# Order of the work on the down-projection's combinations: loads on ScalarE's queue, roundings and stores behind those of a weight unit

## The chip, the cores and the metric

The kernel runs on one core of a Trainium2 chip. Its engines are TensorE (PE: matmuls; its weight loads are listed apart as PEld), VectorE (DVE), ScalarE (ACT), GpSimd (POOL) and SyncE (SP), which here only issues transfers. Each engine works through its own instructions in order: an instruction that waits holds up all that stand behind it on that engine, and that includes transfers which an engine issues. The metric is device time in microseconds (us) of one execution.

## The reference

One layer of a streaming encoder over 512 prompt frames and 64 sample frames, model width 2048: a modulated RMSNorm, two recurrent mixers with their projections, a residual, and then the part that matters here, a gated feed-forward network:

```
gate, val = split(h @ w_up)                   # 2048 -> 2 x 5632
act = silu(causal_dwconv(gate) + bias) * val  # width 3
x = x + g2 * (act @ w_down)                   # 5632 -> 2048
```

and a last RMSNorm. Everything is float32.

## The kernel before, in words

**Products.** A float32 product is made of three matmuls in a rounded format: the weight is split into a high part `wh` (ScalarE rounds it, line 1628) and a low part `wl` (VectorE subtracts, line 1629), the activations likewise, and PE adds wh·hi, wh·lo and wl·hi (lines 1722 to 1724). On top of that the two large products of the network use a scheme with seven block products in place of eight (steps c = 0 to 6): each step multiplies one combination of four weight blocks by one combination of four activation blocks.

**Units.** `up` walks through 44 units t of the up-projection (128 output channels of gate and of value each) and then 32 units of the down-projection. An up unit has 7 steps of 24 matmuls, 168 in all; a down unit has 7 steps of 15, 105 in all. `up_prep` makes the weights of a step two steps ahead of its product: it forms the combination on VectorE (the tiles `s`), rounds it on ScalarE and splits it (`up_split`). The buffers of `wh` and `wl` are three deep, so ScalarE can round a weight only once PE is done with the one three back. `up_load` loads the four weight blocks a11, a21, a22, a12 of a unit into tiles `raw` on SP's queue; six of these rotate in the up-projection. `up_out` takes a step's result from PSUM; `up_conv` and `up_act` make the gated activations of a unit one unit later, and store them in DRAM (`actd[t]`, line 1780).

**The combinations.** The first 40 activation tiles feed the down-projection in 20 pairs. While the up-projection runs, `pair_put(p)` loads `actd[2p]` and `actd[2p + 1]` back into tiles `j`, forms four combinations on GpSimd (tiles ta and tb, line 1849), rounds all seven on ScalarE in four instructions (line 1853), makes the low parts on GpSimd (line 1849 again) and stores both parts in DRAM tiles `cd[p]` (lines 1858 and 1859). The down-projection loads them into freed places (`fill`, line 1901), five per step. `pair_put` is a generator: `up` advances it by one piece at chosen steps. A pair begins at step 3 of an even unit and is advanced at 12 of the next 15 steps.

**What sets the order.** The text of the program sets the order in which work is offered; a scheduler then places each instruction on its engine at the place where, by its own estimate of durations, it can go first. `issue_after(x)` pins the instructions inside it behind instruction x where both are on the same engine. In the kernel before, `split_of` (a unit's subtraction on VectorE) is used so, but nothing of `pair_put` is pinned.

**The end.** In the last eight down units `down_end` adds the partial sums on GpSimd (lines 1945 and 1947), scales them by a modulation vector on ScalarE (line 1954) and adds the residual on GpSimd (line 1955), one piece at each of four steps.

In the down-projection four of the six tiles `j` join the rotation of `raw` tiles, which makes ten, and the other two become places for combinations.

## Time and profile before

| | us |
|---|---|
| median of three runs | 2889.24 (2886.13 to 2890.58) |
| the profiled execution | 2888.42 |
| its span in the profile | 2886.7 |
| up-projection, units 3 to 41 | 1338.1 to 2295.8 |
| down-projection, first to last unit | 2341 to 2810 |

In rows of instructions the columns are start, duration, engine, line of the kernel, operation, tiles (out<-in; the numbers of the buffers are left out) and, in brackets, how long the engine had been idle and what ended that. Rows of stretches give for each engine its busy time and the number of its instructions, then TensorE's granted clock, the share of the DMA engines and GB/s.

### The profile page before, as it was taken

Reading aid. Unit: us, or ns where it says so; the run is one execution under the profiler, and the core shown is the slowest. Engines: PE = TensorE matmul, PEld = TensorE weight load, DVE = VectorE, ACT = ScalarE, POOL = GpSimd, SP = SyncE. Lnnn points to the kernel's source line nnn. Section 1 sums busy time; section 2 is a strip of 40 time slices with the busy share of each in tenths; the row PEclk is TensorE's granted clock in tenths of the full one; section 3 lists DMA queues with packets and bytes.
Section 4 is the critical chain, followed back from the end, with each engine's and each line's share of the span. In section 5 each row is a group of like instructions: output and inputs, shape, how many; then the busy total and the mean of one; then the engine's idle time right before and its main releaser. Section 6 shows DMA issues by size and latency. Waiting matters only on the chain.

```text
span 2886.7 us, 52859 instructions
## 1 busy us (share of the span) xinstructions
PE 2771.4 (96%) x20612; PEld 2671.4 (93%) x20612; DVE 2277.2 (79%) x3721; ACT 1307.3 (45%) x2314; POOL 471.7 (16%) x453
## 2 busy tenths in 40 slices
PE   7999999999999999999999999999999999999988
PEld 4799999999989999999999999999999999999987
DVE  4578787787877887678888888888888876888876
ACT  4255555454544342554444444444444444333343
POOL 0001000010000000002323333333323200000340
PEclk9999999999999999999999999999999999999999
DMA  9965445455554577524555545455545574673651
GB/s 306 317 195 162 134 137 148 136 166 160 155 155 124 151 205 210 158 90 146 157 152 150 157 146 166 142 161 148 161 142 160 170 251 151 183 237 104 216 155 66
DMA packets 647197, 478.18 MB, mean 166 GB/s; under 512 B 65929, under 2 KB 574084, under 8 KB 646948
## 3 DMA queue, kind: packets, MB, share of 16 engines
q1 hardware_dynamic: 639604, 473.14, 55.0%
q8 instruction: 162, 2.65, 0.4%
q10 hardware_dynamic: 7344, 1.67, 0.3%
q14 instruction: 87, 0.71, 0.1%
HBM read 397.76 MB, written 76.96 MB: 164 GB/s over the span
## 4 chain that ended last, share of the span: by engine, by line
PE 39%; issue 22%; DVE 20%; DMA 9%; ACT 5%; POOL 5%; SPq 0%; ACTq 0%; DVEq 0%; POOLq 0%
PE g L646 17%; PE g L648 8%; DVE wl L1629 5%; PE bank L2220 4%; DMA actd<-v 4%; ACT wh L1628 2%; DVE acc L2204 2%; POOL j L1849 2%; PE bank L1724 2%; DVE ca L1772 2%; PE bank L1722 2%; PE bank L1723 2%; DVE s L1656 2%; DMA j<-actd 2%; PE bank L2216 1%
## 5 line engine op out<-in xcount | busy, mean ns | idle before, releaser
L1724 PE MATMUL bank<-slot,wl 128*128 128x290 f32 (+1 forms) x3024 | 901.4, 298 | 51.1 <-DVE wl L1629 51.0
L1722 PE MATMUL bank<-slot,wh 128*128 128x290 f32 (+1 forms) x3024 | 902.8, 299 | 3.3 <-ACT wh L1628 1.7
L1723 PE MATMUL bank<-slot,wh 128*128 128x290 f32 (+1 forms) x3024 | 903.4, 299 | 0.0
L1724 PEld LDWEIGHTS bank<-slot,wl 128*128 128x128 f32 x3024 | 576.7, 191 | 66.4 <-DVE wl L1629 66.4
L1722 PEld LDWEIGHTS bank<-slot,wh 128*128 128x128 f32 x3024 | 569.3, 188 | 9.3 <-issue 3.3
L1723 PEld LDWEIGHTS bank<-slot,wh 128*128 128x128 f32 x3024 | 574.2, 190 | 0.1
L646 PE MATMUL g<-hh,wh 128*128 128x288 f32 x2048 | 472.7, 311 | 1.0 <-ACT ts L2204 0.8
L648 PE MATMUL g<-hh,wl 128*128 128x288 f32 x2048 | 442.3, 297 | 1.7 <-DVE wl L1026 1.7
L646 PE MATMUL g<-hl,wh 128*128 128x288 f32 x2048 | 442.3, 297 | 0.0
L1628 ACT ACTIVATE wh<-raw 128x1024 fp32r<-128x1024 f32 (+1 forms) x304 | 279.8, 921 | 326.9 <-PE bank L1723 234.9
L1629 DVE TENSOR_TENSOR wl<-raw,wh 128x1024 fp32r<-128x1024 f32 (+1 forms) x304 | 322.0, 1059 | 95.5 <-ACT wh L1628 93.0
L646 PEld LDWEIGHTS g<-hh,wh 128*128 128x128 f32 x2048 | 325.0, 190 | 21.8 <-issue 15.1
L648 PEld LDWEIGHTS g<-hh,wl 128*128 128x128 f32 x2048 | 330.8, 189 | 5.3 <-issue 3.3
L646 PEld LDWEIGHTS g<-hl,wh 128*128 128x128 f32 x2048 | 330.1, 189 | 3.6 <-issue 2.7
L1629 DVE TENSOR_TENSOR wl<-s,wh 128x1024 fp32r<-128x1024 f32 (+1 forms) x228 | 275.1, 1208 | 65.0 <-ACT wh L1628 64.4
L1628 ACT ACTIVATE wh<-s 128x1024 fp32r<-128x1024 f32 (+1 forms) x228 | 209.7, 921 | 206.3 <-PE bank L1723 74.4
L1849 POOL TENSOR_TENSOR j<-j,j 128x288 f32<-128x288 f32 (+2 forms) x140 | 202.4, 1463 | 225.4 <-DMA j<-actd 218.2
L2204 ACT ACTIVATE wh<-raw 128x1024 fp32r<-128x1024 f32 x135 | 142.7, 1057 | 198.4 <-PE g L646 192.6
L2204 DVE SCALAR_TENSOR_TENSOR acc<-aw,ct,acc 128x512 f32<-128x512 f32 x284 | 201.1, 742 | 4.5 <-DMA aw<-in_w_ada_dram 4.5
L2204 DVE TENSOR_TENSOR wl<-raw,wh 128x1024 fp32r<-128x1024 f32 x135 | 165.0, 1222 | 46.0 <-ACT wh L2204 43.4
L1722 PE MATMUL g<-slot,wh 128*128 128x288 f32 x560 | 168.5, 301 | 8.1 <-DVE slot L1924 7.3
L1723 PE MATMUL g<-slot,wh 128*128 128x288 f32 x560 | 166.0, 297 | 0.0
(341 smaller groups left out, 4071.8 us busy)
## 6 DMA issues: line engine op xcount, KB each, us to landing
raw<-in_w_up_dram SPq DMA_DIRECT2D x176, 512.0 KB
raw<-in_w_in_dram SPq DMA_DIRECT2D x100, 512.0 KB
raw<-in_w_down_dram SPq DMA_DIRECT2D x128, 320.0 KB
aw<-in_w_ada_dram SPq DMA_DIRECT2D x79, 512.0 KB
slot<-cd SPq DMA_DIRECT2D x140, 288.0 KB
cd<-j SPq DMA_DIRECT2D x120, 288.0 KB
xr<-in_w_ada_dram SPq DMA_DIRECT2D x49, 512.0 KB
hraw<-in_w_ada_dram SPq DMA_DIRECT2D x40, 512.0 KB
```

The costliest lines, as they stand in the source:

```text
L646: T.matmul(ps[:, h if bank is None else bank, :n], wh, x[:, h, :n], start=f, stop=False)
L648: T.matmul(ps[:, h if bank is None else bank, :n], wl, ah[:, h, :n], start=False, stop=stop)
L1628: self.nc.scalar.activation(hi, src, AF.Copy)
L1629: self.nc.vector.tensor_tensor(lo, src, hi.bitcast(F32), op=ALU.subtract)
L1656: V.tensor_tensor(s2, g("s1"), g("a11"), op=ALU.subtract)
L1722: T.matmul(ps, wh[:, j], hi, start=(c < 3 and j == 0), stop=False, skip_group_check=True)
L1723: T.matmul(ps, wh[:, j], lo, start=False, stop=False, skip_group_check=True)
L1724: T.matmul(ps, wl[:, j], hi, start=False, stop=(j == n - 1), skip_group_check=True)
L1772: V.scalar_tensor_tensor(ca[:, :578], cb[:, j:j + 578], w, ca[:, :578], op0=ALU.mult, op1=ALU.add)
L1849: minus = lambda out, a, b: G.tensor_tensor(out, a, b, op=ALU.subtract)
L2204: return f(*a, **kw)
L2220: return self.engine.matmul(out, *a, **kw)
```

## The change

Six things are altered.

1. The loads of a pair go on ScalarE's DMA queue, two whole tiles in place of one whole and two halves on SP's queue. They are pinned behind the rounding that was offered last (`round_of`).
2. A pair begins one unit later, at step 1 of an odd unit, with its loads. The four combinations follow at step 2, and the roundings and stores at steps 1, 2, 4, 5 and 6 of the even unit after it (`PAIR_STEPS`).
3. Each of the four roundings is pinned behind the rounding of a unit's weight that was offered last, and each store behind the last weight load (`load_of`). Rounding and subtraction are offered for r0 and r1 first, then ta, then tb.
4. The rounded parts get tiles of their own (j4, j5, j6; the high part of r0 goes into the second half of r0), so `j` has seven tiles and not six. In the down-projection two of them join the `raw` tiles, which makes eight in place of ten, and five become places for combinations.
5. With fewer `raw` tiles, the load of blocks a11 and a21 two units ahead is offered at step 5 and not at step 3 of a down unit.
6. In `down_end` the residual is loaded in two pieces without its gap, so that one addition on GpSimd does for both pieces; the scalings on ScalarE are pinned behind the last rounding.

```
-            if t + 2 < N_UNITS:
-                self.up_load(t + 2, ("a11", "a21"))
         elif c == 4: ...
         elif c == 5:
...
+            if t + 2 < N_UNITS:
+                self.up_load(t + 2, ("a11", "a21"))
...
-                self.raws[0:0] = [(self.xp, f"j{n}") for n in range(4)]
-                self.vacant += [(self.xp, f"j{n}") for n in (4, 5)]
+                self.raws[0:0] = [(self.xp, f"j{n}") for n in range(2)]
+                self.vacant += [(self.xp, f"j{n}") for n in range(2, 7)]
...
-                if t % 2 == 0 and 2 <= t <= 2 * NJ * NCH and c == 3:
-                    job = self.pair_put(t // 2 - 1)
-                    for d in (2, 3, 4, 5, 7, 9, 10, 11, 12, 13, 14, 15):
-                        self.at_step.setdefault(k + d, []).append(job)
-                for job in self.at_step.pop(k, ()):
-                    next(job, None)
+                if t % 2 and 3 <= t <= 2 * NJ * NCH + 1 and c == 1:
+                    self.pair = self.pair_put(t // 2 - 1)
+                if (t % 2, c) in PAIR_STEPS and self.pair:
+                    next(self.pair, None)
...
+        def split(src, hi):
+            with self.tc.issue_after(self.round_of):
+                nc.scalar.activation(hi, src, AF.Copy)
+            minus(src.bitcast(F32R), src, hi.bitcast(F32))
+        def put(lo, hi, c):
+            with self.tc.issue_after(self.load_of):
+                nc.sync.dma_start(cd[:, c, 0], hi)
+                nc.sync.dma_start(cd[:, c, 1], lo)
+        r0, r1 = tile(F32, 0), tile(F32, 1)
+        with self.tc.issue_after(self.round_of):
+            for s, r in enumerate((r0, r1)):
+                nc.scalar.dma_start(r, self.actd[2 * p + s])
+        yield
+        ta, tb = tile(F32, 2), tile(F32, 3)
+        minus(ta[:, 0], r0[:, 1], r0[:, 0])
+        minus(tb[:, 0], r1[:, 1], r0[:, 1])
+        minus(ta[:, 1], r1[:, 1], ta[:, 0])
+        minus(tb[:, 1], r1[:, 0], ta[:, 1])
+        yield
+        split(r0[:, 0], r0[:, 1].bitcast(F32R))
+        h1 = tile(F32R, 4)
+        split(r1, h1)
+        yield
+        ha = tile(F32R, 5)
+        split(ta, ha)
+        yield
+        put(r0[:, 0], r0[:, 1], B11)
+        put(r1, h1.bitcast(F32), slice(B21, B22 + 1, 2))
+        hb = tile(F32R, 6)
+        split(tb, hb)
+        yield
+        put(ta, ha.bitcast(F32), slice(T1, T2 + 1))
+        yield
+        put(tb, hb.bitcast(F32), slice(T3, T4 + 1, 2))
...
-        xt = [self.v_tile() for _ in range(2)]
+        xt = [self.v_tile()[:, :, :HT] for _ in range(2)]
         for n in range(2):
-            nc.sync.dma_start(xt[n], self.xd[u + n * NPAIR])
+            for z, q in ((slice(0, HP), slice(0, HP)), (slice(HP, HT), slice(ZS, HZ))):
+                nc.sync.dma_start(xt[n][:, :, z], self.xd[u + n * NPAIR][:, :, q])
...
-            for z, q, f in ((slice(0, HP), slice(0, HP), 0), (slice(HP, HT), slice(ZS, HZ), 1)):
-                A.activation(x[:, :, z], x[:, :, z], AF.Copy, scale=self.mod[:, 5, m, f:f + 1])
-                G.tensor_tensor(x[:, :, z], x[:, :, z], xt[n][:, :, q], op=ALU.add)
+            with self.tc.issue_after(self.round_of):
+                for z, f in ((slice(0, HP), 0), (slice(HP, HT), 1)):
+                    A.activation(x[:, :, z], x[:, :, z], AF.Copy, scale=self.mod[:, 5, m, f:f + 1])
+            G.tensor_tensor(x, x, xt[n], op=ALU.add)
```

How instructions move, at pair 8 (`actd[16]` and `actd[17]`, printed as actd_152 and actd_153; its combinations are cd_124). First ScalarE before, from the rounding for step 6 of unit 18 to that for step 2 of unit 19. `wh<-` are roundings of weights (`s` a combination made on VectorE, `raw` a loaded block); the four of line 1853 are pair 8's, ta and tb first (j_19698, j_19699), then r0 and r1:

```order
L1628 ACTIVATE wh_19594<-raw_19272 128x1024
L1628 ACTIVATE wh_19626<-raw_19448 128x1024
L1853 ACTIVATE j_19847<-j_19698 128x576
L1853 ACTIVATE j_19918<-j_19699 128x576
L1628 ACTIVATE wh_19666<-s_19630 128x1024
L1853 ACTIVATE j_19996<-j_19664 128x288
L1758 ACTIVATE cb<-g_19557 128x512
L1759 ACTIVATE cb<-g_19557 128x64
L1853 ACTIVATE j_20070<-j_19700 128x576
L1761 ACTIVATE ca_19660<-cb,cols 128x578
L1628 ACTIVATE wh_19703<-s_19670 128x1024
```

And after, in unit 20 (lines are up to three higher; j_19751 and j_19752 are r0 and r1, j_19794 and j_19795 are ta and tb):

```order
L1737 ACTIVATE p_2802_19969<-bank_19938 128x290
L1853 ACTIVATE j_19751<-j_19751 128x288
L1853 ACTIVATE j_20003<-j_19752 128x576
L1776 ACTIVATE ca_19894<-ca_19894,cols 128x578
L1630 ACTIVATE wh_20007<-raw_19686 128x1024
L1853 ACTIVATE j_20045<-j_19794 128x576
L1630 ACTIVATE wh_20049<-s_19902 128x1024
L1630 ACTIVATE wh_20078<-raw_19760 128x1024
L1853 ACTIVATE j_20112<-j_19795 128x576
L1630 ACTIVATE wh_20115<-raw_19934 128x1024
L1630 ACTIVATE wh_20155<-s_20119 128x1024
```

The four roundings left the place between the roundings for steps 0 and 1 of a unit and now stand, one unit later, after the copy of step 0's result (line 1737 `p`) and between the roundings for steps 4 to 6. The loads stand on ScalarE in unit 19:

```order
L1630 ACTIVATE wh_19721<-raw_19504 128x1024
L1737 ACTIVATE p_2770_19719<-bank_19688 128x290
L1864 DMA j_19751<-actd_152 128x576
L1864 DMA j_19752<-actd_153 128x576
L1776 ACTIVATE ca_19640<-ca_19640,cols 128x578
L1630 ACTIVATE wh_19756<-raw_19427 128x1024
```

They were not on this engine before; now the activation function of the convolution (line 1776) and all roundings that follow are queued behind them. SP's queue for the same pair before, where `raw<-` are weight loads:

```order
L1780 DMA actd_153<-v_19367 256x1x256
L1780 DMA actd_153<-v_19367 256x1x32
L1867 DMA j_19700<-actd_153 128x288
L1871 DMA j_19700<-actd_153 128x288
L1615 DMA raw_19707<-in_w_up_dram 128x8x128
L1858 DMA cd_124<-j_19847 128x2x288
L1859 DMA cd_124<-j_19698 128x2x288
L1858 DMA cd_124<-j_19918 128x2x288
L1859 DMA cd_124<-j_19699 128x2x288
L1858 DMA cd_124<-j_19996 128x288
L1859 DMA cd_124<-j_19664 128x288
L1858 DMA cd_124<-j_20070 128x2x288
```

and after:

```order
L1783 DMA actd_155<-v_19858 256x1x256
L1783 DMA actd_155<-v_19858 256x1x32
L1858 DMA cd_124<-j_19751 128x288
L1859 DMA cd_124<-j_19751 128x288
L1858 DMA cd_124<-j_20003 128x2x288
L1859 DMA cd_124<-j_19752 128x2x288
L1858 DMA cd_124<-j_20045 128x2x288
L1859 DMA cd_124<-j_19794 128x2x288
L1858 DMA cd_124<-j_20112 128x2x288
L1859 DMA cd_124<-j_19795 128x2x288
L1616 DMA raw_20193<-in_w_up_dram 128x8x128
L1616 DMA raw_20269<-in_w_up_dram 128x8x128
```

The loads are gone from SP, the eight stores stand together, one unit later, and a weight load (a11 of the unit after next) that stood ahead of them stands behind them. Last, ScalarE in `down_end` before, for output tiles 2 and 10 (slot_26473 and slot_26474; lines 1954):

```order
L1628 ACTIVATE wh_30613<-s_30571 128x640
L1954 ACTIVATE slot_26473<-slot_26473,mod 128x2x256
L1628 ACTIVATE wh_30639<-s_30569 128x640
L1954 ACTIVATE slot_26473<-slot_26473,mod 128x2x32
L1628 ACTIVATE wh_30664<-raw_30448 128x640
L1954 ACTIVATE slot_26474<-slot_26474,mod 128x2x256
L1954 ACTIVATE slot_26474<-slot_26474,mod 128x2x32
L1628 ACTIVATE wh_30690<-raw_30329 128x640
```

and after, the same two tiles:

```order
L1630 ACTIVATE wh_30626<-raw_30408 128x640
L1630 ACTIVATE wh_30648<-raw_30337 128x640
L1953 ACTIVATE slot_26433<-slot_26433,mod 128x2x256
L1953 ACTIVATE slot_26433<-slot_26433,mod 128x2x32
L1630 ACTIVATE wh_30672<-s_30532 128x640
L1630 ACTIVATE wh_30696<-raw_30506 128x640
L1953 ACTIVATE slot_26434<-slot_26434,mod 128x2x256
L1953 ACTIVATE slot_26434<-slot_26434,mod 128x2x32
L1630 ACTIVATE wh_30723<-raw_30406 128x640
```

The scalings stood after the roundings for steps 2 and 3 of a unit; they stand now after those for step 4 and for step 0 of the next unit, three roundings later. VectorE's order is the same up to unit 43, and TensorE's up to the first down unit.

More of the change, by code (lines that the diff above doesn't have):

```diff
@@ L1621, in up_load @@
                 self.nc.sync.dma_start(raw, w.rearrange("(j s p) n -> s p j n", s=2, p=P)[half])
+            self.load_of = self.nc.cur_bb.bb.instructions[-1]
             self.a[t, n] = raw
@@ L1792, in up @@
         self.t2s = {}
-        self.dn, self.vacant, self.pending, self.sums, self.sums_place, self.at_step = {}, [], [], {}, [], {}
+        self.dn, self.vacant, self.pending, self.sums, self.sums_place, self.pair = {}, [], [], {}, [], None
         self.closing = iter(())
```

30 lines of the change are left out of this document (2 added, 28 removed).

## The prediction

> **What bounds the kernel.** I read the page's head first, then the stretches by time, then the waits inside the pair stretch, then the engines' rows over two units.
>
> ```profile
> span 2886.7 us, 52859 instructions
> PE 2771.4 (96%) x20612; PEld 2671.4 (93%) x20612; DVE 2277.2 (79%) x3721; ACT 1307.3 (45%) x2314; POOL 471.7 (16%) x453
> ```
>
> TensorE is the bound, and only its idle or stretched time can be won. The stretches say where that is: all pair work; an even unit (18); an odd one (19); unit 43, which has no pair work; clean down units; the last seven down units with the entry and exit.
>
> ```profile
> 1338.10:2295.80 957.70, 907.36 (x6554) 888.56 (x6554) 806.80 (x899) 433.68 (x551) 318.73 (x275) 1.00 0.52 155
> 1706.70:1729.40 22.70, 22.70 (x170) 22.70 (x169) 18.84 (x23) 8.82 (x11) 8.04 (x7) 1.00 0.43 121
> 1729.40:1755.40 26.00, 23.93 (x170) 22.81 (x169) 22.76 (x25) 13.29 (x18) 9.57 (x10) 1.00 0.61 183
> 2318.50:2341.20 22.70, 22.70 (x171) 22.70 (x170) 18.77 (x26) 9.49 (x12) 2.43 (x4) 1.00 0.96 348
> 2400.00:2450.00 50.00, 50.00 (x376) 49.66 (x375) 32.47 (x45) 23.43 (x44) 0.00 (x0) 1.00 0.47 147
> 2694.00:2810.00 116.00, 104.54 (x737) 99.70 (x737) 94.30 (x130) 53.32 (x89) 51.75 (x43) 0.99 0.51 145
> ```
>
> The same 170 matmuls take 22.7 us in unit 18 and in unit 43, and 26.0 in unit 19. The first row holds 39 units (3 to 41): 957.7 − 39 × 22.7 = 72.4 us lost, in its 20 odd units 3.6 each. At the clean down rate, 376 matmuls in 50.0 us, the last row's 737 would need 98.0: 18 us lost. Everything the change touches lies in these two sums. Who ends the waits in the first:
>
> ```profile
> PE bank L1724 <- DVE wl L1629: 49.0, 59, 1.5
> ACT j L1853 <- POOL j L1849: 127.2, 58, 5.6
> ```
>
> TensorE waits for VectorE's low parts, about three times in each of 20 units; ScalarE stands 127 us at pair roundings whose input GpSimd hasn't made. ScalarE's rows over the two units:
>
> ```profile
> 1710.03 1.06 ACT L1628 ACTIVATE wh<-raw 128x1024 fp32r<-128x1024 f32 x1 [0.95 <-PE bank L1723]
> 1711.00 0.39 ACT L1734 ACTIVATE p<-bank 128x290 f32<-128x290 f32 x1
> 1712.98 0.78 ACT L1773 ACTIVATE ca<-ca,cols 128x578 f32<-128x578 f32 x1 [1.59 <-DVE ca L1772]
> 1713.67 1.04 ACT L1628 ACTIVATE wh<-raw 128x1024 fp32r<-128x1024 f32 x1
> 1716.58 1.06 ACT L1628 ACTIVATE wh<-s 128x1024 fp32r<-128x1024 f32 x1 [1.87 <-PE bank L1723]
> 1719.77 1.06 ACT L1628 ACTIVATE wh<-raw 128x1024 fp32r<-128x1024 f32 x1 [2.13 <-PE bank L1723]
> 1723.01 1.06 ACT L1628 ACTIVATE wh<-raw 128x1024 fp32r<-128x1024 f32 x1 [2.18 <-PE bank L1723]
> 1727.78 0.69 ACT L1853 ACTIVATE j<-j 128x576 fp32r<-128x576 f32 x1 [3.71 <-POOL j L1849]
> 1729.52 0.69 ACT L1853 ACTIVATE j<-j 128x576 fp32r<-128x576 f32 x1 [1.05 <-POOL j L1849]
> 1730.12 1.05 ACT L1628 ACTIVATE wh<-s 128x1024 fp32r<-128x1024 f32 x1
> 1731.13 0.45 ACT L1853 ACTIVATE j<-j 128x288 fp32r<-128x288 f32 x1
> 1734.56 0.69 ACT L1853 ACTIVATE j<-j 128x576 fp32r<-128x576 f32 x1 [2.13 <-POOL j L1849]
> ```
>
> The rounding at 1730.12, for step 1 of unit 19, stands behind two pair roundings. In VectorE's rows its subtraction follows:
>
> ```profile
> 1705.57 1.22 DVE L1629 TENSOR_TENSOR wl<-s,wh 128x1024 fp32r<-128x1024 f32 x1
> 1712.87 1.21 DVE L1629 TENSOR_TENSOR wl<-raw,wh 128x1024 fp32r<-128x1024 f32 x1
> 1714.74 1.22 DVE L1629 TENSOR_TENSOR wl<-raw,wh 128x1024 fp32r<-128x1024 f32 x1 [0.29 <-ACT wh L1628]
> 1731.19 2.38 DVE L1629 TENSOR_TENSOR wl<-s,wh 128x1024 fp32r<-128x1024 f32 x1 [1.39 <-ACT wh L1628]
> 1737.41 1.21 DVE L1629 TENSOR_TENSOR wl<-s,wh 128x1024 fp32r<-128x1024 f32 x1
> ```
>
> The step 1 part was done 0.1 us into clean unit 18 (1705.57 + 1.22 against 1706.7), and 4.2 us into unit 19 (1733.57 against 1729.4), where the step begins at 3.2 (22.7 / 7). Two causes add up: 2.9 us late start, 1.2 us longer. The longer part coincides with GpSimd:
>
> ```profile
> 1725.01 9.22 POOL L1849 TENSOR_TENSOR j<-j,j 128x288 f32<-128x288 f32 x6 [10.88 <-DMA j<-actd]
> 1735.44 1.43 POOL L1849 TENSOR_TENSOR j<-j,j 128x576 fp32r<-128x576 f32 x1
> ```
>
> **The change, part by part.** Times below are microseconds after a unit's start, from unit 18's rows (start 1706.7).
>
> *Roundings moved (gain).* They come one unit after the loads, when the combinations are long made, so ScalarE no longer stands there; they fall into its gaps. r0 and r1 (0.45 + 0.69) follow the copy `p`, at 4.7, and end at 5.8; the function of line 1773 starts at 6.3 because VectorE ends its wait. ta (0.69) falls into the 1.87 us before the rounding at 9.9, tb (0.69) into the 2.18 before the one at 16.3. Cost on the path 0. Were that cover gone, 0.69 us would come off a lead of about 3 us.
>
> *Loads on ScalarE.* The nearest price is the same engine's stores in this trace:
>
> ```profile
> L1231 ACTq DMA_DIRECT2D sd_g<-ts x8: 326/326/387, 245.7 to 690.1; - x8
> ```
>
> Two per pair, 0.65 us, at 4.7 in the odd unit, in the same gap of 1.59: cost 0. They wait for the stores of actd and for those of the previous pair that free j0 and j1. When those land comes from SP's rows:
>
> ```profile
> 1716.66 1.19 SPq L1780 DMA_DIRECT2D actd<-v  x2
> 1722.67 0.34 SPq L1867 DMA_DIRECT2D j<-actd  x1
> ```
>
> actd goes out 10 us into the even unit and has landed within 6 (a load there had waited for it); the new load is asked for at 22.7 + 4.7 = 27.4, some 11 us after. The previous pair's stores go out from 10 to 17 of that pair's even unit, 10 us ahead of the loads even for the last. Behind a waiting load would stand the function of line 1773 and the roundings; SP loses three loads per pair (about 1.1 us) in a queue that waits anyway. The data is there, by the 2.3 us between the load at 1722.67 and GpSimd at 1725.01 to about 6, at 7 to 11; nobody but GpSimd waits.
>
> *GpSimd's work.* Seven of a pair's eight instructions took 10.7 us above (the first ran in the unit before); the amount stays. Over that time VectorE lost about 4 us per pair (22.76 − 18.84 busy in the two unit rows). Afterwards the four combinations run from about 9 to 14 of the odd unit and the low parts from 5 to 8.5 (r0, r1), near 10 and near 15 of the even unit. VectorE has 3.9 us free per unit (22.7 − 18.84), and from 10 to 17 the roundings it lives on wait for TensorE (the three brackets of about 2 us), so work there is absorbed. The tight place is the low part for step 3: done at 7.4 (1712.87 + 1.21), needed at 9.7 (3 × 3.24), a lead of 2.3. At 4 us lost per 10.7 us of GpSimd, 3.3 us of it take 1.2. Cost 0, bounded by 0 and 20 × 1 = 20 us if VectorE is blocked for all of it (below).
>
> *Stores pinned, order on SP.* Eight issues after the actd store; the a11 load behind them is for the unit after next, so it stands about 22 us ahead of its use. Cost 0; unless a store waits for GpSimd some 20 us it shows nowhere.
>
> So the up-projection gains 72.4, which is also the most it can; the other bound is 52.4.
>
> *Seven `j` tiles, eight `raw` tiles, load offered at step 5.* The down rows show TensorE full with ten tiles. With eight, the load of a22 must wait for step 6 of the unit before last; from that to its use remain about 10 us, against the 2.3 to 6 us a load took above. Three more places for combinations help at the group edges, where loads come in bursts: three of 288 KB at the 348 GB/s of unit 43's row are 2.5 us, at three edges 7; two tiles fewer can cost as much there. I take 0; bounds: 7 us either way.
>
> *`down_end`.*
>
> ```profile
> ACT slot L1954 <- POOL slot L1947: 22.4, 8, 3.3
> ACT slot L1954 <- POOL slot L1945: 15.3, 8, 3.3
> L1955 POOL TENSOR_TENSOR slot<-slot,v 128x512 f32<-128x512 f32 x16 | 20.0, 1249 | 13.1 <-ACT slot L1954 13.1
> L1955 POOL TENSOR_TENSOR slot<-slot,v 128x64 f32<-128x64 f32 x16 | 13.1, 821 | 0.0
> L1947 POOL TENSOR_TENSOR slot<-slot,slot 128x576 f32<-128x576 f32 x8 | 16.0, 2002 | 6.0 <-DVE slot L1924 6.0
> ```
>
> ScalarE waits 37.7 us in 16 places, with weight roundings behind. Three roundings later the sums are made and the waits go. GpSimd's two additions (1.25 + 0.82) become one of 576 (2.0): nothing gained. Sixteen more issues on SP (at 0.34, 5.4 us over 110) are covered by its waits. What GpSimd costs VectorE stays, about 7 us of GpSimd per 14 us unit, and VectorE is 65 to 80% busy here. Of 18 us I take 12; bounds 0 and 18.
>
> Sum: 72.4 + 12 = 84.4 off the profiled 2888.4, so 2804.0. The median of the runs is 0.8 higher: **2805**.
>
> **Rivals.** *VectorE is blocked outright by GpSimd (A).* For: 1.22 became 2.38 at 1731.19. If VectorE does nothing for all 3.3 us of r0's and r1's subtraction, the low part for step 3 comes at 10.7 and not 9.7: 1 us per pair, 20 us in all, and no more than half the gain in `down_end`: 2888.4 − 52.4 − 6 = 2830. Against: above, VectorE lost 4 us in 10.7. [...] Chance 0.13.
>
> *`down_end` gives nothing (B)*, because what GpSimd takes from VectorE decides there: 2888.4 − 72.4 = 2816, or 2817 on the median. Chance 0.15.
>
> *The loads hold up ScalarE (C, slower).* Place: step 1 of each odd unit. A load that waits holds the rounding for step 4, whose low part leads by 3.7 us (done at 1714.74 + 1.22, so 9.3, needed at 4 × 3.24). To lose more than is gained (84.4 / 20 = 4.2 us per pair) the wait must exceed 1.6 + 4 + 4.2, about 10 us beyond 27.4, stores landing 21 us after issue where 6 was seen. Each further us costs 20: with 12 us, 2929. Chance 0.03.
>
> *The down-projection starves on eight tiles (D):* 2 us in each of 32 units, 64 back: 2869; from 2.6 us per unit it is slower. Against: 10 us of lead. Chance 0.03. That the pins do nothing is excluded by the order. Rest, no change at all: 0.01.
>
> **How the numbers follow.** Forecast 0.65, A 0.13, B 0.15, C 0.03, D 0.03, no change 0.01. The range 2792 (all 18 us of `down_end` and 7 at group edges) to 2830 (A) holds the forecast's own 2792 to 2812, B and A. About 0.2%, 6 us, is what a measurement here can tell from no change. Faster: forecast, A, B and most of D, 0.95; same 0.01; slower 0.04.
>
> **What would show it.** Right: odd units of 22.7 us, the matmuls of the pair stretch in about 885 us; no row in which ScalarE waits for GpSimd at line 1853; VectorE's step 3 parts ending by 9 us; ScalarE's loads issuing without a wait in front; no wait of line 1953 for GpSimd of 2 us. Wrong: a rounding that follows a load late (C); TensorE waiting for the low part of step 3 in even units (A); VectorE waiting for `raw` in down units (D). The forecast falls by most if stalls of the size of the old ones come back in the even units, where the roundings now stand.

## The result

The changed kernel takes 2809.74 us (median of four runs, 2807.95 to 2813.45) against 2888.80 for the kernel before, measured beside it: a ratio of 0.973, 95% interval 0.971 to 0.975. Its profiled execution took 2809.85 us with a span of 2808.1. The forecast was 2805, so 84 us less; 79 came.

The head of its page, and the same six stretches as before, in the places where the units now lie (units 3 to 41; even unit 18; odd unit 19; unit 43; clean down units; the last seven):

```profile
span 2808.1 us, 52899 instructions
PE 2748.1 (98%) x20612; PEld 2668.6 (95%) x20612; DVE 2285.0 (81%) x3721; ACT 1314.0 (47%) x2314; POOL 458.7 (16%) x437
```

```profile
1339.10:2227.10 888.00, 888.00 (x6556) 885.52 (x6555) 808.52 (x899) 434.86 (x545) 311.47 (x275) 1.00 0.55 164
1680.50:1703.40 22.90, 22.90 (x171) 22.77 (x170) 21.31 (x25) 12.21 (x16) 9.09 (x8) 1.00 0.60 185
1703.40:1726.00 22.60, 22.60 (x169) 22.60 (x169) 20.11 (x24) 10.12 (x12) 6.93 (x8) 1.00 0.50 144
2249.80:2272.50 22.70, 22.70 (x171) 22.70 (x170) 16.12 (x22) 7.80 (x9) 2.28 (x3) 1.00 1.03 368
2400.00:2450.00 50.00, 50.00 (x376) 49.78 (x375) 42.03 (x66) 19.12 (x26) 0.00 (x0) 1.00 0.56 160
2624.90:2729.50 104.60, 100.38 (x738) 98.09 (x737) 96.30 (x128) 54.45 (x88) 44.39 (x28) 1.00 0.56 152
```

The 39 units of the first row take 888.0 us and not 957.7, and the profile shows TensorE busy in all of it. (The ends of its matmuls are modelled there, so a pause as short as 0.15 us, which comes back below, does not show in this figure.) VectorE's 808.52 is what it was (806.80): the time it loses to GpSimd wasn't saved, it lies elsewhere. Over two units it was 18.84 + 22.76 = 41.6 us busy, now 21.31 + 20.11 = 41.4.

Who ended ScalarE's waits in the pair stretch, the two largest; the old wait of line 1853 for GpSimd (127.2 us) has no row any more, and for TensorE there is no row at all:

```profile
ACT wh L1630 <- PE bank L1726: 249.2, 156, 2.2
ACT wh L1630 <- DVE s L1643: 95.4, 38, 2.5
```

ScalarE's rows in even unit 20 (it starts at 1726.0), with the four roundings of the pair, line 1853 (the first row of it holds two):

```profile
1729.34 1.06 ACT L1630 ACTIVATE wh<-raw 128x1024 fp32r<-128x1024 f32 x1 [0.95 <-PE bank L1726]
1730.31 0.39 ACT L1737 ACTIVATE p<-bank 128x290 f32<-128x290 f32 x1
1730.60 1.01 ACT L1853 ACTIVATE j<-j 128x288 fp32r<-128x288 f32 x2
1732.83 0.78 ACT L1776 ACTIVATE ca<-ca,cols 128x578 f32<-128x578 f32 x1 [1.22 <-DVE ca L1775]
1733.52 1.04 ACT L1630 ACTIVATE wh<-raw 128x1024 fp32r<-128x1024 f32 x1
1734.46 0.67 ACT L1853 ACTIVATE j<-j 128x576 fp32r<-128x576 f32 x1
1735.89 1.06 ACT L1630 ACTIVATE wh<-s 128x1024 fp32r<-128x1024 f32 x1 [0.76 <-PE bank L1726]
1740.05 0.67 ACT L1853 ACTIVATE j<-j 128x576 fp32r<-128x576 f32 x1
```

They fill gaps and wait for nothing, as forecast. Where the time went, from the first matmul of each unit in the profiled execution (us; "rest" is all before unit 3; the matmuls of the down-projection are cut into 32 stretches of 105, in the order in which they ran, and these are the down units of the table and of all that follows, counted from 1):

```
                           rest   units 3-43  down 1  down 2-25  last seven  after them   span
before                     1338.1   1003.1     13.94    338.9      116.1       76.7      2886.7
the change                 1339.1    933.4     15.33    337.1      104.6       78.6      2808.1
```

Of 78.6 us of span, 69.7 are from the up-projection, 11.5 from the last seven down units, 1.8 from down units 2 to 25; 1.4 went in the first down unit, and 2.9 in the rest and after the last unit. The rest column and the time after the last unit vary between 1336 and 1342 and between 76.7 and 80.6 over all runs below, with no pattern that I could assign. The reading below therefore goes by units, each from the one profiled execution of its kernel. An up unit without a stall takes 22.69 us in every kernel. Units 3 to 43 take 933.4 us in all four kernels that keep the order of the change there, and 930.2 in the four that remove what its even units still lose; in the three that keep the stalls of before the same sum varies between 1001.7 and 1003.5.

### The profile page after: what moved, and what is told of

Its sections match the earlier page's. It is cut to its first block, busy times and chain, and to the rows that moved or that the text cites. A ratio compares the mean times of both kernels' runs of the same rounds, so it can differ in the third digit from the quotient of the medians.

```text
span 2808.1 us, 52899 instructions
## 1 busy us (share of the span) xinstructions
PE 2748.1 (98%) x20612; PEld 2668.6 (95%) x20612; DVE 2285.0 (81%) x3721; ACT 1314.0 (47%) x2314; POOL 458.7 (16%) x437
## 3 DMA queue, kind: packets, MB, share of 16 engines
q8 instruction: 162, 2.65, 0.4%
## 4 chain that ended last, share of the span: by engine, by line
PE 81%; DVE 8%; DMA 4%; issue 3%; ACT 2%; POOL 1%; SPq 0%; ACTq 0%; DVEq 0%; POOLq 0%
PE g L647 17%; PE bank L1726 14%; PE bank L1725 14%; PE bank L1727 14%; PE g L649 8%; PE bank L2219 4%; PE g L1725 2%; PE g L1727 2%; PE g L1726 2%; DVE acc L2203 2%; PE bank L2215 1%; PE bank L869 1%; DVE wl L1632 1%; DVE wl L2203 1%; DVE m L2179 1%
## 5 line engine op out<-in xcount | busy, mean ns | idle before, releaser
L1632 DVE TENSOR_TENSOR wl<-raw,wh 128x1024 fp32r<-128x1024 f32 (+1 forms) x304 | 371.4, 1222 | 73.0 <-ACT wh L1630 69.4
L647 PEld LDWEIGHTS g<-hh,wh 128*128 128x128 f32 x2048 | 325.2, 190 | 21.8 <-issue 15.1
L1632 DVE TENSOR_TENSOR wl<-s,wh 128x1024 fp32r<-128x1024 f32 (+1 forms) x228 | 250.4, 1100 | 14.5 <-ACT wh L1630 13.5
L2203 DVE TENSOR_TENSOR wl<-raw,wh 128x1024 fp32r<-128x1024 f32 x135 | 164.8, 1222 | 47.1 <-ACT wh L2203 44.3
L1849 POOL TENSOR_TENSOR j<-j,j 128x288 f32<-128x288 f32 (+1 forms) x120 | 184.4, 1543 | 85.6 <-ACT j L1853 83.1
```

Source lines behind the costliest of these rows:

```text
L647: T.matmul(ps[:, h if bank is None else bank, :n], wh, x[:, h, :n], start=f, stop=False)
L1632: self.nc.vector.tensor_tensor(lo, src, hi.bitcast(F32), op=ALU.subtract)
L1849: minus = lambda out, a, b: G.tensor_tensor(out, a, b, op=ALU.subtract)
L2203: return f(*a, **kw)
```

## The experiments

My theory at the start was the prediction's: what ScalarE does in which order decides. The rivals were the later start, the queue of the loads, the pinned stores and the tiles.

### `down_end` alone, both ways

The changed kernel with the old function; and the kernel before with the new one, that is with the same lines the other way round (`round_of` is set there as in the change).

```
-        xt = [self.v_tile()[:, :, :HT] for _ in range(2)]
+        xt = [self.v_tile() for _ in range(2)]
...
-            with self.tc.issue_after(self.round_of):
-                for z, f in ((slice(0, HP), 0), (slice(HP, HT), 1)):
-                    A.activation(x[:, :, z], x[:, :, z], AF.Copy, scale=self.mod[:, 5, m, f:f + 1])
-            G.tensor_tensor(x, x, xt[n], op=ALU.add)
+            for z, q, f in ((slice(0, HP), slice(0, HP), 0), (slice(HP, HT), slice(ZS, HZ), 1)):
+                A.activation(x[:, :, z], x[:, :, z], AF.Copy, scale=self.mod[:, 5, m, f:f + 1])
+                G.tensor_tensor(x[:, :, z], x[:, :, z], xt[n][:, :, q], op=ALU.add)
```

> The changed kernel with the old `down_end` put back (its scalings not held behind a unit's rounding, one transfer of x per row instead of two, four additions instead of two). Theory (the order on ScalarE: a scaling that waits for GpSimd stands ahead of a weight rounding): the last seven down units lose again what they lost before, 11.5 us of it (116.05 us before, 104.6 us after), so about 2809.7 + 11 = 2821 us, and the waits of the scaling for GpSimd come back on ScalarE. Rival (the gain in the last units came from the pair work being out of the way, or from the load order that eight raw tiles give): no change, 2810 us.

> The kernel before with the new `down_end` alone. PE's and VectorE's orders stay as they are row for row; only ScalarE, GpSimd and the DMA issues on SP move. Theory (the two parts add up and do not touch): 2888.8 - 11 = 2878 us, the up-projection's units as long as before (26.3 us each odd one). Rival (the last units also need the eight raw tiles or the shifted pair work): 2885 to 2889 us.

Measured: with the old function put back 2817.19 us, ratio 0.975 (0.974 to 0.977), against 0.973 for the whole change; with the new one put in alone 2881.85 us, 0.997 (0.996 to 0.998). By units: put back, the last seven take 112.4 us (104.6 with the change); put in alone, 104.3 (116.1 before). ScalarE's waits in the changed kernel with the old function, last seven units:

```profile
ACT slot L1951 <- POOL slot L1944: 17.1, 7, 3.3
ACT slot L1951 <- POOL slot L1942: 16.7, 8, 3.3
```

The mechanism holds: the 33.8 us of waits come back with the function and go with it. It is worth 7.8 us there and 11.8 here; so 3.7 of the 11.5 come with either the function or the rest of the change. Inside the function the pin of the scalings and the single addition were changed together; which of them counts is not shown.

### Roundings not held back

```
-            with self.tc.issue_after(self.round_of):
-                nc.scalar.activation(hi, src, AF.Copy)
+            nc.scalar.activation(hi, src, AF.Copy)
```

> The changed kernel with the roundings of `pair_put` not held behind the unit's rounding; loads, stores, steps and tiles stay. ScalarE then runs r0, r1, ta and tb in one group where its planner puts them, ahead of the weights' roundings of the even unit, and each sooner than GpSimd needs it. Theory A (the order of the roundings is what matters, wherever their operands are): the even units stall again on a rounding that stands in front of a weight's, by 2 to 4 us each, 20 units, so 2850 to 2890 us. Rival B (it is the start one unit later that matters: the operands are long there, so a rounding in any place waits for nothing and costs only its own 0.67 us): 2808 to 2818 us.

Measured: 2807.09 us (2806.54 to 2808.53), ratio 0.971 (0.970 to 0.973). My theory A fell. Odd and even units take 22.69 us, units 3 to 43 930.2: 3.2 us less than with the pins. ScalarE's rows (line 1852 is the pair's rounding; odd unit 19 starts at 1701.1, its loads were issued at 1704.63):

```profile
1708.04 1.04 ACT L1630 ACTIVATE wh<-raw 128x1024 fp32r<-128x1024 f32 x1
1708.99 0.67 ACT L1852 ACTIVATE j<-j 128x576 fp32r<-128x576 f32 x1
1711.04 0.45 ACT L1852 ACTIVATE j<-j 128x288 fp32r<-128x288 f32 x1 [1.39 <-POOL j L1849]
1712.25 0.69 ACT L1852 ACTIVATE j<-j 128x576 fp32r<-128x576 f32 x1 [0.76 <-POOL j L1849]
1713.14 0.69 ACT L1852 ACTIVATE j<-j 128x576 fp32r<-128x576 f32 x1 [0.20 <-POOL j L1849]
1713.73 1.04 ACT L1630 ACTIVATE wh<-s 128x1024 fp32r<-128x1024 f32 x1
```

Rival B isn't right in its reason either. ScalarE does still stand at pair roundings that wait for GpSimd, 2.35 us here, and a weight waits behind them. It costs nothing, and the lead shows why. Lead is the time from the end of a weight's low part on VectorE to the matmul that first uses it, the mean over 19 or 20 units. The first row is for comparison: in those units the pair's work falls behind the roundings of all seven steps, and its leads are those of unit 43, which has no pair work:

```
step                                          0    1    2    3    4    5    6
late, held loads (below), odd              4.4  3.5  3.1  2.7  4.0  4.3  4.4
before, odd                                 4.4  0.1  0.1  0.1  1.8  2.7  4.3
the change, even                            4.4  3.5  3.1  0.9  1.7  2.6  4.3
roundings not held back, odd                4.4  3.5  3.1  2.7  4.0  1.1  2.0
```

A hold of some 3 us in front of step 5's weight comes off a lead of 4.3. Before, the same kind of wait stood in front of step 1's, which has 3.5, was longer (3.7 + 1.05 us in the rows of unit 19), and took all of it and 3.6 us more. This run alone does not say whether the place or the length counts: by the leads, a hold of 3.2 us (4.3 − 1.1) would have fitted in front of step 1 too (an estimate from the table).

### The pins in the kernel before

```
-            nc.scalar.activation(hi[:, k], src[:, k], AF.Copy)
+            with self.tc.issue_after(self.round_of):
+                nc.scalar.activation(hi[:, k], src[:, k], AF.Copy)
```

> The kernel before, its steps, loads and stores as they were, with one thing added: the five roundings of `pair_put` held behind the unit's own rounding. Theory A (order on ScalarE alone): most of the 72 us of the odd units go, 2816 to 2830 us. Rival B (the later start, or loading on ScalarE's queue, is needed: the loads still land late, so a rounding still waits for GpSimd, only a little further down the row): 2850 to 2889 us, with ScalarE waiting for GpSimd in front of another weight. Rival C (VectorE loses to GpSimd on its own account): more than 2889 us where the subtractions now fall on steps in which VectorE has more to do.

(`round_of` is set there as in the change.) Measured: 2841.33 us (2837.2 to 2845.91), ratio 0.983 (0.982 to 0.985), between the two. Units 3 to 43 fall from 1003.1 to 956.0, so the place of the roundings alone is worth 47.1 of 69.7 us. (It is four instructions per pair that are held, not five.) ScalarE has no wait for GpSimd at them any more. What is left are pauses of TensorE between steps 3 and 4: 1.1 us in 15 of the 20 even units, 0.7 in 9 of the 20 odd ones. TensorE's waits, then one of the longer pauses (unit 18), with step 4's weight on ScalarE, VectorE's rows beside it and the matmul that ends it:

```profile
PE bank L1723 <- ACT wh L1628: 14.6, 15, 1.0
PE bank L1723 <- DVE g L1741: 5.1, 10, 0.5
```

```profile
1694.33 1.04 ACT L1628 ACTIVATE wh<-raw 128x1024 fp32r<-128x1024 f32 x1
1696.55 2.66 DVE L1780 SCALAR_TENSOR_TENSOR v<-v,ca 128x512 f32<-128x512 f32 x2
1699.13 0.45 DVE L1741 TENSOR_TENSOR g<-bank,p 128x290 f32<-128x290 f32 x1
1699.73 0.37 PE L1723 MATMUL bank<-slot,wh 128*128 128x290 f32 x1 [0.97 <-ACT wh L1628]
```

The profile names ScalarE's rounding, but that had ended 4.4 us before. What ended 0.15 us before TensorE went on, here and at all the other pauses, is `g`: it reads the bank (the part of PSUM into which the matmuls add) that step 4 then writes. In front of it stand the products `v`, 2.66 us here and 0.94 us in unit 20 with the change. The pauses come to 23.7 us, nearly all of the 25.8 by which units 3 to 43 still exceed 930.2. So what the pins alone do not bring is no wait of ScalarE but the bank at which, with the change, 0.15 us per even unit is still lost (below). Which other part of the change brings VectorE there earlier is not shown.

### The queue of the loads, and their pin

Three studies. In the first the loads are on SP's queue, held behind the last weight load:

```
-        with self.tc.issue_after(self.round_of):
+        with self.tc.issue_after(self.load_of):
             for s, r in enumerate((r0, r1)):
-                nc.scalar.dma_start(r, self.actd[2 * p + s])
+                nc.sync.dma_start(r, self.actd[2 * p + s])
```

> The changed kernel with the two loads of a pair on SP's queue again, issued behind the last weight load that stands before them, at the same step (the odd unit's step 1). Theory (the queue is of no matter as long as the loads land some 10 us before GpSimd reads them, two steps on; SP's waits in front of them are short): 2808 to 2814 us. Rival (SP's queue waits for a weight tile in front of these loads, they land late, GpSimd's four subtractions slide into the even unit onto VectorE's full steps, and the roundings wait for them): 2830 to 2860 us.

Measured: 2811.2 us, ratio 0.973 (0.972 to 0.974); units 3 to 43 take 933.4 us, to the tenth what they take with ScalarE's queue. In this kernel the queue is of no matter, as long as the loads are held.

In the second they stay on ScalarE's queue, without the `issue_after`:

```
-        with self.tc.issue_after(self.round_of):
-            for s, r in enumerate((r0, r1)):
-                nc.scalar.dma_start(r, self.actd[2 * p + s])
+        for s, r in enumerate((r0, r1)):
+            nc.scalar.dma_start(r, self.actd[2 * p + s])
```

> The changed kernel with its two loads per pair still on ScalarE's queue but not held behind a rounding; roundings and stores stay pinned. The planner then puts them forward by ten weight roundings, into the even unit before, close behind the store of the second of the two activations. Theory (what decides is how long after that store the load is asked for: asked for too early it holds ScalarE, in order, until the store has landed, some 6 us, with weight roundings behind it that lead by about 4): 1 to 3 us lost in each of 20 units, 2830 to 2870 us, and ScalarE waiting for the DMA of actd. Rival (the pins of the roundings are what counts): 2808 to 2812 us.

Measured: 2846.25 us (2843.86 to 2847.72), ratio 0.985 (0.984 to 0.986); the odd units but the first take 24.7 us, and units 3 to 43 971.5, 38.1 more than with the pin. What the loads wait for was not what I had named:

```profile
ACT wh L1630 <- DMA cd<-j: 108.9, 30, 5.0
PE bank L1727 <- DVE wl L1632: 23.0, 42, 1.3
```

They hold ScalarE until the stores of the previous pair have freed the tiles (`cd<-j`), up to 5 us, with weights behind, whose lead at steps 2 and 3 falls to 0.1. This is the mechanism of the prediction's rival C, with shorter waits and another cause.

In the third, the kernel before gets only the later offer and held loads, on SP:

```
-                        self.at_step.setdefault(k + d, []).append(job)
+                        self.at_step.setdefault(k + d + min(7, 43 - t), []).append(job)
...
-        nc.sync.dma_start(r0, self.actd[2 * p])
+        with self.tc.issue_after(self.load_of):
+            nc.sync.dma_start(r0, self.actd[2 * p])
```

and so for both halves of r1 (`load_of` is set there as in the change).

> The kernel before with its pairs offered one unit later and only its loads held behind the last weight load, all on SP's queue; roundings and stores are left to the planner, `down_end`, tiles and the weight loads are those of before. (Offered one unit later without the pin, no row of any engine changes its place.) Theory (a load that is asked for long after the activations' store lands at once, GpSimd's combinations are there when ScalarE's row comes to their rounding, and nothing else of the change is needed for the up-projection): odd units fall from 26.3 to 22.7 or 23.2 us, 2816 to 2828 us. Rival (the new split of the work over the steps, both loads first and r0, r1 ahead of ta and tb, is needed too, since the loads still come in three pieces over three steps with the roundings close behind): 2845 to 2890 us.

Measured: 2912.61 us (2907.86 to 2915.36), ratio 1.008 (1.006 to 1.009): slower than before, outside both expectations. (Offered later without the pin, four rows on SP change places at the last pair, and no other row of any engine.) Odd units are clean; even units take 27.3 us. ScalarE at unit 18 (it starts at 1713.1; line 1854 is the pair's rounding), one of TensorE's longest waits, the sum of these waits in the pair stretch, and two stretches around this one:

```profile
1709.36 0.69 ACT L1854 ACTIVATE j<-j 128x576 fp32r<-128x576 f32 x1 [4.86 <-POOL j L1850]
```

```profile
1719.69 0.40 PE L1725 MATMUL bank<-slot,wl 128*128 128x290 f32 x1 [2.78 <-DVE wl L1630]
```

```profile
PE bank L1725 <- DVE wl L1630: 51.7, 20, 2.8
```

```profile
1716.00:1720.00 4.00, 1.22 (x8) 0.85 (x7) 4.00 (x4) 2.64 (x5) 3.02 (x3) 1.00 0.53 180
1720.00:1726.00 6.00, 6.00 (x35) 6.00 (x34) 5.95 (x8) 3.55 (x5) 0.91 (x2) 0.72 0.35 106
```

The loads go out later, and the planner puts the roundings close behind them again, ahead of the weights of steps 0 and 1. A wait of 4.9 us there leaves these two a lead of 0.6 and 0.1 us, and TensorE stands 2.8 us. The wait is not all of it: from 1711.03 to the end of step 1's low part VectorE works without a gap, and three of its rows take longer than alone (1.2 us), with GpSimd busy beside them (3.84 of 4 us from 1712 to 1716, 3.02 of 4 from 1716 to 1720):

```profile
1711.03 1.78 DVE L1630 TENSOR_TENSOR wl<-raw,wh 128x1024 fp32r<-128x1024 f32 x1 [3.76 <-ACT wh L1629]
1712.73 2.44 DVE L1641 TENSOR_TENSOR s<-raw,raw 128x1024 f32<-128x1024 f32 x1
1717.22 2.42 DVE L1630 TENSOR_TENSOR wl<-s,wh 128x1024 fp32r<-128x1024 f32 x1
```

So a later start does not help by itself, when it leaves the wait in front of the same weights.

### Stores not held back

```
-            with self.tc.issue_after(self.load_of):
-                nc.sync.dma_start(cd[:, c, 0], hi)
-                nc.sync.dma_start(cd[:, c, 1], lo)
+            nc.sync.dma_start(cd[:, c, 0], hi)
+            nc.sync.dma_start(cd[:, c, 1], lo)
```

> The changed kernel with the stores of the combinations not held behind a weight load. SP then issues some of them between the weight loads, and a store waits there for GpSimd with loads queued behind it. Theory (stores as the change has them cost nothing, and unpinned they hold a weight load by up to a few us, which the raw tiles absorb): 2810 to 2820 us. Rival (the pin of the stores carries a part of the gain): 2830 us and more, with roundings of weights waiting for their DMA.

Measured: 2809.09 us, ratio 0.973 (0.971 to 0.974): no difference from the change by the whole time. By units there is one: the first down unit takes 13.93 us, as before, and not 15.33. In all six kernels with the stores held it took 15.0 to 16.2, in all three without 13.93. ScalarE waits there for the weights' transfer, 1.7 us with the change, 0.4 us without the pin:

```profile
ACT wh L1630 <- DMA raw<-in_w_down_dram: 1.7, 1, 1.7
```

```profile
ACT wh L1630 <- DMA raw<-in_w_down_dram: 0.4, 1, 0.4
```

That wait is not the whole account: it is 1.7 us as well in two other kernels with held stores, whose first down unit took 15.8 and 16.2. The edit also changes the scheduler's order at this place: 12 rows on VectorE, 8 on ScalarE and 22 matmuls stand elsewhere. With the change VectorE reads a result (line 1921) ahead of the low parts for which TensorE then waits, and itself waits for that result:

```profile
2285.00 0.46 DVE L1921 TENSOR_TENSOR slot<-bank,slot 128x288 f32<-128x288 f32 x1 [1.46 <-PE bank L1727]
2285.38 1.55 DVE L1632 TENSOR_TENSOR wl<-raw,wh 128x640 fp32r<-128x640 f32 x2
```

Which share the late transfer has and which the order is not shown.

### Eight `raw` tiles in the kernel before

```
-                self.raws[0:0] = [(self.xp, f"j{n}") for n in range(4)]
-                self.vacant += [(self.xp, f"j{n}") for n in (4, 5)]
+                self.raws[0:0] = [(self.xp, f"j{n}") for n in range(2)]
+                self.vacant += [(self.xp, f"j{n}") for n in (2, 3, 4, 5)]
```

> The kernel before with two, not four, of the j tiles given to the raw weight tiles of the down-projection and four, not two, to the combinations: eight raw tiles as the change has. Prediction's view (eight are as good as ten): 2886 to 2891 us. Rival (the weights of the first down unit, and of the last ones, come late with eight tiles; the changed kernel lost 1.4 us in the first down unit and 1.9 us in the final phase): 2891 to 2898 us.

Measured: 2890.04 us, ratio 1.000 (0.999 to 1.001). No difference by the whole time, and the first down unit is 13.98: the tiles aren't its cause. By units two differences cancel: down units 2 to 25 take 1.8 us more, the last seven 2.3 us less. Down units 10 and 18, each the second of a group of eight, take 15.8 us (15.1 before, 14.1 with the change). What makes them clean in the changed kernel, 2 us in all, stays open.

### What the even units still lose

With the change TensorE pauses once per even unit, 0.15 us, between steps 3 and 4. VectorE's and TensorE's rows of unit 20 there; `g` (line 1743) reads the bank that step 4's first matmul, the last row, writes to:

```profile
1735.46 2.26 DVE L1632 TENSOR_TENSOR wl<-raw,wh 128x1024 fp32r<-128x1024 f32 x1
1737.65 0.94 DVE L1782 SCALAR_TENSOR_TENSOR v<-v,ca 128x512 f32<-128x512 f32 x2
1738.51 0.45 DVE L1743 TENSOR_TENSOR g<-bank,p 128x290 f32<-128x290 f32 x1
```

```profile
1739.10 0.37 PE L1725 MATMUL bank<-slot,wh 128*128 128x290 f32 x1
```

The low part for step 4 (2.26 us beside GpSimd, 1.22 alone) was ready 1.4 us ahead. The study lets `g` go ahead of `v`:

```
             V.tensor_tensor(self.g[:, 1], y, self.p1, op=ALU.add)
+            self.g_of = nc.cur_bb.bb.instructions[-1]
...
-            if 0 < t < NFF and c == 2 or t == NFF and c == 1:
+            if t == NFF and c == 1:
...
                 self.up_out(t, c)
+                if t and c == 2:
+                    with self.tc.issue_after(self.g_of):
+                        self.up_act(t - 1, self.v, self.ca)
```

> The changed kernel with VectorE's order swapped at one place: the two activation products of the unit before (`up_act`) are held behind the sum that reads the second bank (`g`), at step 2 of every unit. PE's and ScalarE's orders stay row for row. Theory (the 0.15 us that each even unit still loses between steps 3 and 4 is PE waiting for that bank, which VectorE reads late because GpSimd slowed it in steps 1 and 2): 20 x 0.15 = 3 us less, 2806.5 us, and even units of 22.69 us. Rival (it is the weight's low part, or the clock): 2809 to 2811 us, even units stay at 22.85.

Measured: 2810.1 us (2803.18 to 2811.84), ratio 0.972 (0.971 to 0.973). Units 3 to 43 take 930.2 us and even units 22.69, 3.2 less, as the theory has it; the low part of step 4 is as long as before:

```profile
1737.05 2.27 DVE L1632 TENSOR_TENSOR wl<-raw,wh 128x1024 fp32r<-128x1024 f32 x1
1739.24 0.45 DVE L1743 TENSOR_TENSOR g<-bank,p 128x290 f32<-128x290 f32 x1
```

TensorE's and ScalarE's rows stand in the same order in both kernels, so the 0.15 us were that bank. In the whole time it doesn't show: this profile's rest is 2.9 us and its first down unit 0.9 us longer than the change's.

### Two versions that beat both

Without the pins on roundings and on stores, the two edits above together:

```
-            with self.tc.issue_after(self.round_of):
-                nc.scalar.activation(hi, src, AF.Copy)
+            nc.scalar.activation(hi, src, AF.Copy)
...
-            with self.tc.issue_after(self.load_of):
-                nc.sync.dma_start(cd[:, c, 0], hi)
-                nc.sync.dma_start(cd[:, c, 1], lo)
+            nc.sync.dma_start(cd[:, c, 0], hi)
+            nc.sync.dma_start(cd[:, c, 1], lo)
```

> The changed kernel with neither the roundings nor the stores of `pair_put` held back; the loads stay pinned on ScalarE's queue. Theory (of the pins only that of the loads carries the gain; each of the other two costs a little: the roundings' 0.16 us in each even unit, the stores' 1.4 us in the first down unit): 2809.7 - 3.2 - 1.4 = 2805 us, even units of 22.69 us, first down unit of 13.9 us. Rival (one of the two is needed when the other is gone): 2812 us or more.

Measured: 2804.92 us (2803.16 to 2805.99), ratio 0.971 (0.969 to 0.972); even units 22.69, first down unit 13.93. The two add as expected. The interval still overlaps that of the change; the units that differ do not: 930.2 against 933.4 us and 13.93 against 15.33.

The same with `down_end`'s last piece on VectorE:

```
-            with self.tc.issue_after(self.round_of):
+            with self.tc.issue_after(self.split_of):
                 for z, f in ((slice(0, HP), 0), (slice(HP, HT), 1)):
-                    A.activation(x[:, :, z], x[:, :, z], AF.Copy, scale=self.mod[:, 5, m, f:f + 1])
-            G.tensor_tensor(x, x, xt[n], op=ALU.add)
+                    nc.vector.scalar_tensor_tensor(x[:, :, z], x[:, :, z], self.mod[:, 5, m, f:f + 1],
+                                                   xt[n][:, :, z], op0=ALU.mult, op1=ALU.add)
```

> As the kernel without pins on roundings and stores, and in `down_end` the scaling on ScalarE and the residual's addition on GpSimd made into one operation on VectorE (x times the modulation plus the residual, two pieces per row). Theory (in the last seven units, 104.6 us where 98 would do, VectorE reads PE's banks late because GpSimd's additions slow it): GpSimd loses 4 of its 7 us per unit, up to 6 us less, 2800 to 2805 us. Rival (VectorE is the one that is short there, and four more operations on it cost more than GpSimd took): 2806 to 2815 us.

Measured: 2802.91 us (2802.43 to 2803.73), ratio 0.970 (0.969 to 0.972). The last seven units:

```profile
2619.20:2720.90 101.70, 99.37 (x740) 98.11 (x739) 97.28 (x160) 41.79 (x58) 25.73 (x15) 1.00 0.57 156
```

101.7 us, 2.9 less than with the change (which has the same function as the kernel without the two pins). VectorE has 32 more instructions than with the change and is busy only 1 us longer (97.28 against 96.30), beside 25.73 us of GpSimd and not 44.39. TensorE's waits in the last seven units, with the change and here:

```profile
PE g L1725 <- DVE slot L1921: 3.8, 5, 1.6
```

```profile
PE g L1725 <- DVE slot L1919: 2.2, 3, 1.3
```

The scaling left ScalarE at the same time, so the part of GpSimd's addition in the 2.9 us is not shown by itself. The interval of this version, too, touches that of the change; its four runs lie 4.2 us and more below those of the change.

## Why the prediction was right, and where it wasn't

*Up-projection, 72.4 us: 69.7 came.* The reading was right that the loss was the pair roundings that stood on ScalarE in front of weights, and that in the change they would fall into gaps. The reason given, that the combinations are long made by then, is only half of it. The pins on the old schedule, with loads still late, bring 47.1 us, and what they leave is the bank that `g` reads, not ScalarE; without the pin of the roundings, with GpSimd still waited for, all of it comes. What decides is the length of the wait against the lead of the weight behind it: 3.2 of 4.3 us taken without the pin, 3.5 of 3.5 and a stall of 3.6 before. Length and place were not varied one at a time.

*GpSimd's work, cost 0, bounded by 20: 3.2 us.* This is the step whose size was off. The amount stayed and VectorE absorbed nearly all. The loss of 4 us per pair was read against unit 18, which isn't free of GpSimd itself (8.04 us of it). The place was wrong: step 3's low part, named as the tight one, did become the tightest and kept 0.9 of its 2.65 us of lead; what came late was the bank that `g` reads. I had followed VectorE's products to TensorE, and not the banks that VectorE must read before TensorE may write. Rival A (blocked outright, 2830) is refuted in its sum. Single rows here do double (2.26 and 2.45 us in unit 20, where 1.22 is usual), but over two units the sum is far below GpSimd's 16.0 us: 41.4 − 2 × 18.84 = 3.7 us more than two units of unit 18's kind, and about 4.5 us against the undisturbed rows of the same lines (an estimate from the trace: each row of units 18 and 19 less the short rows of the same line and shape).

*Loads on ScalarE, cost 0:* right; the queue makes no difference. Rival C did not come, since the pin puts the loads after the tiles are free; taken away, 1.9 us per pair are lost.

*Stores, cost 0: wrong by 1.4 us.* "Unless a store waits for GpSimd some 20 us it shows nowhere" looked at the a11 load of an up unit. In the first down unit it shows: ScalarE's wait for a transfer is 1.3 us longer than without the pin, and the scheduler orders the engines' rows differently; how much each costs stays open.

*Tiles, 0 ± 7:* eight instead of ten `raw` tiles cost nothing in the kernel before by the whole time; by units, +1.8 and −2.3 us cancel. Rival D is refuted.

*`down_end`, 12 of 18:* the last seven units gained 11.5, the function alone 11.8 in the kernel before. Rival B is refuted. Of the 6 us left 2.9 went when GpSimd's last addition and ScalarE's scaling became one operation on VectorE.

The 84.4 us of the sum and the 78.6 of the span differ by 2.7 in the up-projection, 1.4 in the first down unit and 0.5 in the last seven, less 1.8 gained in down units 2 to 25; the other 2.9 are the stretches before and after, which vary by that. That the total came within 5 us is in part luck: the 1.8 us were not forecast, and the stretches at both ends could as well have fallen the other way.

## What to carry to other kernels

Before an instruction that may wait is put on an engine in order, list the lead of each instruction behind it, and put the wait in front of one whose lead is longer than the wait; to start later does not help by itself, since a scheduler that estimates durations can put the wait right back in front of the same weight. A pin is worth testing one by one: of the three in `pair_put` that of the loads is worth some 38 us here, and the other two cost a little. Where one engine slows another, look at the banks it must free as well as at the data it must deliver, and check the end of the releaser that a profile names: one that ended 4 us before the pause did is not the cause.

## What the runs showed of the hardware

In the kernel with late, held loads most pauses of TensorE cost more than themselves. 19 of its 20 even units have a pause of 2.5 to 3.1 us from one matmul to the next; behind 13 of them 15 to 25 matmuls follow at 0.24 us and not 0.135 (granted clock 0.72 in the row above, of unit 18), behind the other six only 3 (granted clock 1.00 in the row below, of unit 20). The step with the pause takes 7.9 us in unit 18 and 6.2 in unit 20, and 3.24 in a clean unit. In units 3 to 41 of the kernel before, one matmul at 0.24 us follows behind each of the 60 pauses of 0.5 to 1.8 us (also from one matmul to the next); behind one of them, of 1.03 us at 2229.19, 14 more follow from 2230.37 on (granted clock 0.67 from 2229 to 2233), behind the two longest, of 1.81 us, no more. So the length of a pause alone does not say here how many slow matmuls follow; what decides it is not shown.

```profile
1770.00:1776.00 6.00, 5.95 (x45) 5.71 (x44) 5.95 (x8) 3.64 (x5) 0.90 (x2) 1.00 0.33 97
```

What VectorE lost beside GpSimd changed by 1.0 us in two units with where GpSimd's work lay: with all of a pair's in one odd unit VectorE is 20.20 + 20.20 = 40.4 us busy in two units, with it spread over both 41.4, beside 16.5 and 16.0 us of GpSimd. The rows of units 18 and 19 of the kernel with roundings not held back:

```profile
1678.43:1701.12 22.69, 22.69 (x171) 22.69 (x169) 20.20 (x27) 10.99 (x14) 2.74 (x4) 1.00 0.62 192
1701.12:1723.80 22.68, 22.68 (x170) 22.68 (x169) 20.20 (x23) 11.35 (x14) 13.76 (x11) 1.00 0.48 138
```
